# One decoder layer on one core: the order of the value products in attention, and where side b's keys and values lie

## The chip, the cores and the metric

The kernel runs on one core of one Trainium2 chip. The metric is the device time of one execution in microseconds (us); lower is better. Times below come from three timed executions and from one further execution that was profiled. The engines are named as in the profile: PE (TensorE: matmuls; PEld is its weight load), DVE (VectorE), ACT (ScalarE), POOL (GpSimd) and SP (SyncE, which issues the DMAs).

## What is computed

The layer takes 1024 tokens of width 1024. It normalises them, modulates them with a condition vector and projects them with one wide matrix (`w_in`, 5144 columns). Two attentions share the input. **Side a** has 8 heads in 2 groups of 4 that share keys and values; it runs three branches (compressed keys, selected blocks `s`, a window `w` of 512). **Side b** has 8 heads in 2 groups, a window of 128 and a learned sink in the softmax. Their gated outputs are projected, merged, projected again, added to the input and normalised.

```
o_sel = _selected_attention(qa, k_s, v_s, sel_idx)
o_win = _banded_attention(qa, k_w, v_w, NSA_WINDOW)
...
o_b = _banded_attention(qb, k_b, v_b, SWA_WINDOW, sinks[l]).reshape(B, S, SWA_WIDTH)
...
merged = jax.nn.sigmoid(gm_a) * (y_a @ w_up_a[l]) + jax.nn.sigmoid(gm_b) * (y_b @ w_up_b[l])
out = merged @ w_out[l]
```

## The kernel before

The program is written as one stream per stage, and the framework's scheduler then orders the instructions of each engine by its own model of their times. So the order on an engine is not the order in the source.

**Stages.** Until about 145 us of the profiled span the input is normalised and the first projections are made; from there to about 740 us attention runs; then the gates, the two up-projections and the output projection follow.

**Attention** (`Att`, `run` L942 on) goes through 32 units: side a or b, group g, query tile qt of 128 tokens. A unit has one or two branches, a branch a row of key tiles of 128 keys. For each key tile `score` (L887 on) multiplies keys with the queries of 4 heads (two matmuls of 512 columns, `qa` and `qb`), adds a mask on DVE where the tile is an edge (L898), takes the exponentials `e` on ACT (L900, L902), rounds them to 16 bits as `ph` on ACT (L905), and subtracts to get the low part `pl` on POOL (L908). `weigh` (L911) then multiplies the exponentials with the values: for each of 4 heads three small matmuls of 64 or 65 columns, in which `ph` or `pl` is the stationary operand: `ph` with the values' high part, `ph` with their low part, `pl` with the high part. That is 12 matmuls for a key tile, and there are 162 key tiles. `combine` (L922 on) divides and adds up the branches (L930 to L936).

**Fill.** Between these steps `feed` (in `run`) hands out pieces of other projections, called fill below: query projections, the keys and values of side b (`kv_b`), and the gate columns (`gm_block`). Their products write to two PSUM banks (`pj`), which DVE or ACT must empty before the next one starts. All matmuls are issued by the helper `mm`, so they stand under line L107.

**Keys and values.** `new_kv` (L591 on) makes for each branch and each group a tile of keys `K` (fp32, with extra rows that carry masks and the softmax maximum) and a tile of values `V` (16 bits, high and low part and a column of ones). Group 0's tiles for `s` and `w` lie in the pool `kv0`, group 1's in `kv1`. When side a's first 8 units (group 0) are done, `kv_b` (L1261 on) closes `kv0` and opens the pool `kvb` in its place: four new tiles `Kb`, `Vb`, and fixed rows that must be written into them. `block_rows` (L186 on) builds these in a scratch tile `es` (a memset and four affine_selects on POOL, L189 to L196), and `fixed_kv` (L599 on) copies them to both `Kb` and sets the column of ones in both `Vb`. `es` has the tag `vrb`, the same as side b's raw values `vr["b"]` (printed as `vrb`), so the first raw values (L1277) can be written only when the copies from `es` are done. Of the fixed rows, row 80 picks the maximum of the `s` branch from the queries' extra columns; the tile of the `w` branch has a 1 in row 81 only.

Of the kernel before, what the change touches and what calls it, by code (L numbers as in the profile page):

```python
# [7 lines left out]
F32 = mybir.dt.float32  # L8
# [5 lines left out]
OP = mybir.AluOpType  # L14
# [83 lines left out]
class Layer:  # L98
# [492 lines left out]
    def new_kv(self, ps, br, vp):  # L591

        self.K[br] = [p.tile([128, 2, 1024], F32R, name=f"K{br}{g}") for g, p in enumerate(ps)]
        self.V[br] = [p.tile([128, NT, VW], F16, name=f"V{br}{g}") for g, p in enumerate(ps)]
        self.vinv[br] = self.c2.tile([128, 1], F32, name="vinv" + br)
        self.vr[br] = vp.tile([128, NT, 128], F32, name="vr" + br, tag="vr" + br)
        self.vm[br] = vp.tile([128, NT], F32, name="vm" + br)
# [110 lines left out]
class Att:  # L708
# [112 lines left out]
    def M(self, u):  # L821
        L, nc, w = self.L, self.nc, self.w
        side, g, qt = u
        st = self.U[u]
        qa, qbt = st["qa"], st["qbt"]
        brs = self.branches(u)
        mx = w.tile([128, 4, 2, 3], F32, name="mx", tag="mx", bufs=2)
        nc.gpsimd.memset(mx, -3e38)
        if side == "b":
            nc.gpsimd.tensor_copy(mx[:, :, 0, 2], L.sink[:, g * 4:g * 4 + 4])  # L830
        for bi, (br, kts) in enumerate(brs):
            n = 128 * len(kts)
            k0 = 128 * kts[0]
            ns = -(-n // 512)
            cuts = [0] + [min(n, 128 * -(-len(kts) * (i + 1) // ns)) for i in range(ns)]

            groups = []
            for a, b in sorted(zip(cuts, cuts[1:]), key=lambda c: c[0] - c[1]):
                per = 512 // (b - a) if PACK else 1
                groups += [(a, b, range(h, min(4, h + per))) for h in range(0, 4, per)]  # L840
            slots = [0] * 4
            for a, b, hs in groups:
                ps = self.ms.tile()
                for i, h in enumerate(hs):
                    self.last.append(L.mm(ps[:, i * (b - a):(i + 1) * (b - a)], qa[:, h * 128:h * 128 + 128],
                                     L.K[br][g][:, 0, k0 + a:k0 + b], True, True).ins)
                for i, h in enumerate(hs):
                    parts = []
                    if br == "s" and qt >= 4:
                        d = min(b, n - 128)  # L850
                        parts.append((a, d, st["sel"][:, (k0 + a) // 64:(k0 + d) // 64, None].to_broadcast(
                            [128, (d - a) // 64, 64])))
                        if b == n:
                            parts.append((d, b, L.mk[:, 512:640]))
                    elif br == "s" or (br == "w" and qt < 4) or (br == "b" and qt == 0):
                        parts.append((a, b, L.mk[:, 640 - n + a:640 - n + b]))
                    elif br == "w":
                        parts.append((a, b, L.mk[:, a:b]))
                    else:
                        parts.append((a, b, rawap(L.mk, 0, [[512, 2], [1, 128]])))  # L860
                    for c, d, m in parts:
                        if d == c:
                            continue
                        jk = w.tile([128, 512], BF, name="jk", tag="jk")
                        src, o = ps[:, i * (b - a) + c - a:i * (b - a) + d - a], jk[:, :d - c]
                        if len(m.shape) == 3:
                            src = src.rearrange("p (x y) -> p x y", x=m.shape[1])
                            o = o.rearrange("p (x y) -> p x y", x=m.shape[1])
                        nc.vector.tensor_tensor_reduce(o, src, m, 1.0, -3e38, OP.add, OP.max,  # L869
                                                       mx[:, h, bi, slots[h]:slots[h] + 1])  # L870
                        slots[h] += 1
                yield 0.22 * (b - a) * len(hs) / 512
        nc.vector.tensor_reduce(qbt[:, :, 80:82], mx, axis=AX.X, op=OP.max, negate=True)
        if side == "b":
            es = st["es"] = w.tile([128, 2, 4], F32, name="esink", tag="esink", bufs=3)
            nc.gpsimd.tensor_tensor(es[:, 0], L.sink[:, g * 4:g * 4 + 4], qbt.bitcast(F32)[:, :, 80], op=OP.add)
            nc.scalar.activation(es[:, 1], es[:, 0], AF.Exp, bias=L.poff)
        yield 0
        tr = self.ms.tile([128, 4, 128], F32R)
        for h in range(4):  # L880
            self.last.append(nc.tensor.transpose(tr[:, h, :], qbt[:, h, :], L.idr).ins)  # L881
        qb = st["qb"] = w.tile([128, 512], F32R, name="qb", tag="qb", bufs=2)
        nc.scalar.copy(qb, tr.bitcast(F32).rearrange("p h t -> p (h t)"))
        yield 0.25
# [23 lines left out]
        eng.tensor_tensor(pl, e, ph, op=OP.subtract)  # L908
        return ph, pl

    def weigh(self, u, br, kt, first, last, av, ph, pl):  # L911
        L = self.L
        v = L.V[br][u[1]][:, kt, :]
        for h in range(4):
            o = av[:, h * 65:h * 65 + 65]
            hs = slice(h * 128, h * 128 + 128)
            L.mm(o, ph[:, hs], v[:, 0:65], first and h == 0, False)
            L.mm(o[:, 0:64], ph[:, hs], v[:, 65:129], False, False)
            r = L.mm(o, pl[:, hs], v[:, 0:65], False, last and h == 3)
        return r  # L920

    def combine(self, u, bi, av):  # L922
# [19 lines left out]
    def run(self, units, fill, ratio, values):  # L942

        L = self.L
# [30 lines left out]
        steps = []  # L975
# [4 lines left out]
        first = {}  # L980
# [27 lines left out]
        side = "start"  # L1008
# [4 lines left out]
        av = None  # L1013
        si = 0
        emitted = {}
# [7 lines left out]
        for gi, grp in enumerate(groups):  # L1023
            u, bi = steps[grp[0]][:2]
            ui = units.index(u)
            side = "e" if ui < EU else u[0]
            n = ends[ui] - first[u]

            while si <= groups[min(gi + 1, len(groups) - 1)][-1]:
                su = steps[si][0]  # L1030
                finish(self.M, su)
                emitted[si] = self.score(su, steps[si][2], steps[si][3])
                si += 1
                feed(0.43)
            k = grp[-1] - first[u] + 1
            if ui + 1 < len(units):
                part(self.M, units[ui + 1], k, n)
            if ui + 2 < len(units):
                part(self.C, units[ui + 2], k, n)
            if steps[grp[0]][4]:  # L1040
                av = self.av.tile()
            for i in grp:
                br, kt, fst, lst = steps[i][2:]
                w = self.weigh(u, br, kt, fst, lst, av, *emitted.pop(i))
            anchors.append(w.ins)
            feed(0.54 * len(grp))
            if lst:
                self.combine(u, bi, av)
            if k == n:
                if ui + 1 < len(units):  # L1050
                    finish(self.M, units[ui + 1])
                if ui + 2 < len(units):
                    finish(self.C, units[ui + 2])
                self.U.pop(u)
                fill.done(u)
# [51 lines left out]
def run_layer(L):  # L1107
    tc, nc, I = L.tc, L.nc, L.I
# [41 lines left out]
    qp, qp_cm = L.pool("q")  # L1150
# [5 lines left out]
    k1, k1_cm = L.pool("kv1")  # L1156
    k0, k0_cm = L.pool("kv0")
    vp, vp_cm = L.pool("vrows")
# [6 lines left out]
    es = vp.tile([128, 1024], F32, name="es", tag="vrw")  # L1165
# [89 lines left out]
    wk, wk_cm = L.pool("work", 1, side="right")  # L1255
# [3 lines left out]
    kvb = []  # L1259

    def kv_b():  # L1261

        L.close(k0_cm)
        p, cm = L.pool("kvb")
        kvb.append(cm)
        es = p.tile([128, 1024], F32, name="es", tag="vrb")
        L.block_rows(es)
        L.new_kv((p, p), "b", p)
        L.fixed_kv("b", es)
        w = chunk(L.w_in_src(OFF_KVB, 256), 256, eng=lambda: nc.gpsimd)  # L1270
        yield 0
        for t in range(NT):
            a = pj.tile()
            for k in range(KT):
                L.proj(a[:, :256], t, w, ks=[k])
                yield 0.33
            nc.scalar.copy(L.vr["b"][:, t], a[:, 128:256])  # L1277
            L.v_max("b", t)
            L.kv_tail(t, a[:, 0:128], "b", p, A.ms, nc.vector)
        L.v_split("b", A.ms.tile(), p)  # L1280
# [1 line left out]
    fill.kv = kv_b  # L1282
    A.run(units, fill, RATIO, values)
    fill.rest()
    for cm in (wk_cm, kvb[0], k1_cm, qp_cm):
        L.close(cm)


# [3 lines left out]
    wk, wk_cm = L.pool("work2", 2, side="right")  # L1292
# [44 lines left out]
    wk, wk_cm = L.pool("work3", 2, side="right")  # L1337
# [24 lines left out]
    for j in range(KT):  # L1362
        ws = []
        for i, nm in enumerate("ab"):
            src = I["w_up_" + nm].rearrange("l (k p) c -> (l p) k c", p=128)
            w = []
# [133 lines left out]
```

## Time and profile before

| what | value |
|---|---|
| median of 3 timed executions | 966.98 us (966.77 to 968.43) |
| profiled execution, its own time | 970.35 us |
| its span in the profile | 968.6 us |
| PE busy | 932.0 us, 96% of the span |
| POOL, DVE, ACT busy | 607.5, 553.3, 470.9 us |
| matmul instructions in the trace | 6592 |

The profile is of one execution. A matmul's end is modelled, so the start of one matmul to the start of the next tells more than a duration: it is called a slot below. A chain of waits is followed back from the last instruction to what released each step.

### The profile page before, as it was taken

How to read it: one execution, taken by the hardware profiler on the slowest of the kernel's cores; microseconds unless marked ns; L12 is line 12 of the kernel's file. 1: busy time of each engine (PE TensorE's matmuls, PEld its weight loads, DVE VectorE, ACT ScalarE, POOL GpSimd, SP SyncE). 2: the span in 40 equal slices, each digit the busy share in tenths (PEclk: the TensorE clock that was granted, in tenths of full speed). 3: DMA queues.
4: the chain of work that ended last, by engine and by line, in shares of the span. 5: the costliest groups of instructions: out<-in, count | busy, mean ns of one | idle time of the engine just before them, and what ended most of it. 6: DMA issues, size and time to landing. Idle time of an engine off the chain costs nothing.

```text
span 968.6 us, 18679 instructions
## 1 busy us (share of the span) xinstructions
PE 932.0 (96%) x6592; PEld 784.3 (81%) x6592; DVE 553.3 (57%) x1613; ACT 470.9 (49%) x983; POOL 607.5 (63%) x841
## 2 busy tenths in 40 slices
PE   7899999999999999989999999999989989999995
PEld 5789998788898887878899877799768758778885
DVE  7933465544675653466876552455652556554687
ACT  5846334335546556546655466655763544632100
POOL 7867566355758676767777666656753666635733
PEclk8999999999999999999999999999999999999998
DMA  9813222222102122103101222121305948666212
GB/s 333 273 38 113 80 76 71 61 66 78 49 7 62 50 60 67 50 12 88 50 7 40 66 61 66 50 67 39 88 23 186 295 132 244 202 198 223 92 78 97
DMA packets 93278, 95.40 MB, mean 98 GB/s; under 512 B 7616, under 2 KB 72192, under 8 KB 93184
## 3 DMA queue, kind: packets, MB, share of 16 engines
q1 hardware_dynamic: 93184, 94.21, 31.6%
q8 instruction: 52, 0.85, 0.4%
q14 instruction: 42, 0.34, 0.1%
HBM read 73.21 MB, written 20.97 MB: 97 GB/s over the span
## 4 chain that ended last, share of the span: by engine, by line
PE 78%; DVE 6%; POOL 5%; ACT 4%; DMA 4%; issue 3%; POOLq 0%; SPq 0%; DVEq 0%; ACTq 0%
PE bank L107 75%; DMA x<-in_x_dram 1%; POOL rstd L541 1%; DVE res L1433 1%; PE bank L751 1%; PE bank L881 1%; DMA raw<-in_w_up_b_dram 1%; POOL whl L258 1%; POOL pl L908 1%; DMA raw<-in_w_up_a_dram 1%; DMA z<-gm_raw 1%; DVE e L898 1%; DVE stats L1421 1%; DVE z L1420 1%; DVE lnst L531 0%
## 5 line engine op out<-in xcount | busy, mean ns | idle before, releaser
L107 PE MATMUL bank<-whl,uH 128*128 128x256 f32 (+3 forms) x1168 | 271.3, 323 | 5.7 <-ACT uH L448 3.4
L107 PE MATMUL bank<-uH,whl 128*128 128x512 f32 x768 | 252.3, 402 | 0.2 <-DVE cf L931 0.2
L908 POOL TENSOR_TENSOR pl<-e,ph 128x512 f16<-128x512 f32 x162 | 188.5, 1170 | 77.1 <-ACT ph L905 61.1
L107 PEld LDWEIGHTS bank<-whl,uH 128*128 128x128 f32 x1168 | 196.8, 189 | 24.2 <-ACT uH L448 4.4
L107 PE MATMUL bank<-whl,uL 128*128 128x256 f32 (+3 forms) x584 | 182.4, 321 | 0.0
L107 PEld LDWEIGHTS bank<-uH,whl 128*128 128x128 f32 x768 | 141.7, 190 | 27.9 <-PE bank L881 0.5
L107 PE MATMUL bank<-uL,whl 128*128 128x512 f32 x384 | 152.5, 398 | 0.0
L258 POOL TENSOR_TENSOR whl<-raw,whl 128x256 fp32r<-128x256 f32 x128 | 100.2, 791 | 53.6 <-ACT whl L257 46.2
L107 PEld LDWEIGHTS bank<-whl,uL 128*128 128x128 f32 x584 | 109.6, 188 | 8.0
L905 ACT CAST ph<-e 128x512 f16<-128x512 f32 x162 | 98.0, 618 | 28.3 <-PE bank L107 26.2
L869 DVE CUSTOM_DVE_ANT_0 jk<-bank,mk 128x256 bf16<-128x256 f32 (+3 forms) x168 | 73.8, 439 | 32.3 <-PE bank L107 28.9
L902 ACT ACTIVATE e<-bank,poff 128x512 f32<-128x512 f32 x92 | 62.0, 687 | 52.8 <-PE bank L107 45.0
L107 PEld LDWEIGHTS bank<-uL,whl 128*128 128x128 f32 x384 | 72.8, 189 | 15.4
L107 PE MATMUL bank<-yH,whl 128*128 128x512 f32 x256 | 81.9, 402 | 1.7 <-ACT yH L1315 0.8
L257 ACT CAST whl<-raw 128x256 fp32r<-128x256 f32 x128 | 50.9, 402 | 64.8 <-PE bank L107 39.9
L107 PEld LDWEIGHTS <-ph 128*128 128x128 f16 x1296 | 66.1, 97 | 15.1 <-issue 7.6
L898 DVE TENSOR_TENSOR e<-bank,mkt 128x512 f32<-128x512 f32 x70 | 47.5, 688 | 53.1 <-PE bank L107 36.4
L247 POOL TENSOR_TENSOR whl<-raw,whl 128x256 fp32r<-128x256 f32 (+3 forms) x60 | 54.4, 913 | 26.4 <-ACT whl L246 26.2
L107 PEld LDWEIGHTS <-pl 128*128 128x128 f16 x648 | 59.6, 99 | 12.5 <-issue 6.9
L1248 DVE COPY gmo<-bank 128x512 f32<-128x512 f32 x48 | 33.1, 689 | 57.3 <-PE bank L107 50.4
L900 ACT ACTIVATE e<-e,poff 128x512 f32<-128x512 f32 x70 | 49.8, 721 | 32.5 <-DVE e L898 32.3
L246 ACT CAST whl<-raw 128x256 fp32r<-128x256 f32 (+3 forms) x72 | 34.2, 480 | 63.9 <-DMA raw<-in_w_out_dram 35.7
(303 smaller groups left out, 1786.9 us busy)
## 6 DMA issues: line engine op xcount, KB each, us to landing
raw<-in_w_in_dram SPq DMA_DIRECT2D x136, 128.0 KB, 2.2
gm_raw<-gmo SPq DMA_DIRECT2D x48, 256.0 KB, 2.1
wada<-in_w_ada_dram SPq DMA_DIRECT2D x16, 512.0 KB, 6.1
sg<-gm_raw SPq DMA_DIRECT2D x32, 256.0 KB, 3.3
x<-in_x_dram SPq DMA_DIRECT2D x8, 512.0 KB, 5.0
o_raw<-q SPq DMA_DIRECT2D x32, 128.0 KB, 1.9
o<-o_raw SPq DMA_DIRECT2D x8, 512.0 KB, 6.6
z<-gm_raw SPq DMA_DIRECT2D x16, 256.0 KB, 4.9
```

The lines of the kernel that those rows point to most:

```text
L107: return self.nc.tensor.matmul(out, l, r, start=start, stop=stop, skip_group_check=True)
L246: self.cast = nc.scalar.copy(h, raw).ins
L247: low = eng.tensor_tensor(l, raw, h.bitcast(F32), op=OP.subtract).ins
L257: nc.scalar.copy(hl[:, 0], raw)
L258: eng.tensor_tensor(hl[:, 1], raw, hl.bitcast(F32)[:, 0], op=OP.subtract)
L869: nc.vector.tensor_tensor_reduce(o, src, m, 1.0, -3e38, OP.add, OP.max, mx[:, h, bi, slots[h]:slots[h] + 1])
L898: nc.vector.tensor_tensor(e.rearrange("p (h q) -> p h q", h=4), ps.rearrange("p (h q) -> p h q", h=4), L.mkt[:, int(edge), None, :].to_bro ...
L900: nc.scalar.activation(e, e, AF.Exp, bias=L.poff)
L902: nc.scalar.activation(e, ps, AF.Exp, bias=L.poff)
L905: nc.scalar.copy(ph, e)
L908: eng.tensor_tensor(pl, e, ph, op=OP.subtract)
L1248: (nc.scalar.copy if GMC == 2 or GMC == 1 and (b + th) % 2 else nc.vector.tensor_copy)(g, a)
```

## The change

Two things are changed. First, `weigh` takes the list of tiles of a step (here always one), puts for each head the low part `pl` first and then the two products of `ph`, and ties each matmul to follow the one before it (`issue_after`), so that the scheduler keeps the 12 of a key tile together. Second, side b gets no `K` and `V` tiles and no fixed rows of its own: its group 0 uses the tiles of side a's group 0 of branch `s`, and its group 1 those of branch `w`. Since the latter has its 1 in row 81, side b's maximum and sink move to slot `g`. `kv0` stays open to the end of attention, and `kvb` holds the raw values alone, under no shared tag with `es`.

```
+        self.new_v(br, vp)
+
+    def new_v(self, br, vp):
         self.vinv[br] = self.c2.tile([128, 1], F32, name="vinv" + br)
...
-            nc.gpsimd.tensor_copy(mx[:, :, 0, 2], L.sink[:, g * 4:g * 4 + 4])
+            nc.gpsimd.tensor_copy(mx[:, :, g, 2], L.sink[:, g * 4:g * 4 + 4])
...
-    def weigh(self, u, br, kt, first, last, av, ph, pl):
+    def weigh(self, u, br, tiles, first, last, av):
...
+        todo = []
+        for kt, ph, pl in tiles[::-1]:
+            v = L.V[br][u[1]][:, kt, :]
+            for h in range(4):
+                o = av[:, h * 65:h * 65 + 65]
+                hs = slice(h * 128, h * 128 + 128)
+                todo += [(o, pl[:, hs], v[:, 0:65]), (o, ph[:, hs], v[:, 0:65]), (o[:, 0:64], ph[:, hs], v[:, 65:129])]
+        r = None
+        for i, (o, p, v) in enumerate(todo):
+            first_, last_ = first and i == 0, last and i == len(todo) - 1
+            if r is None:
+                r = L.mm(o, p, v, first_, last_)
+            else:
+                with L.tc.issue_after(r.ins):
+                    r = L.mm(o, p, v, first_, last_)
...
-        L.close(k0_cm)
         p, cm = L.pool("kvb")
...
-        es = p.tile([128, 1024], F32, name="es", tag="vrb")
-        L.block_rows(es)
-        L.new_kv((p, p), "b", p)
-        L.fixed_kv("b", es)
+        L.new_v("b", p)
+        L.K["b"], L.V["b"] = ([x[br][0] for br in "sw"] for x in (L.K, L.V))
```

What the scheduler makes of it on two engines. On PE, the start of a key tile's value products in side a's second group, before (`Vs`, `Ks`, `Kw` are values and keys, `qa`, `qb`, `qat` queries, `bank` a PSUM bank):

```order
L107 LDWEIGHTS ph
L107 MATMUL bank_6254<-Vs_931,ph 128x65
L107 LDWEIGHTS ph
L107 MATMUL bank_6254<-Vs_931,ph 128x64
L107 MATMUL bank_6355<-qa,Kw_936 128x512
L107 MATMUL bank_6355<-qb,Kw_936 128x512
L107 MATMUL bank_6296<-Ks_929,qa 128x512
L107 LDWEIGHTS pl
L107 MATMUL bank_6254<-Vs_931,pl 128x65
```

and the same tile with the change:

```order
L754 MATMUL bank_6310<-idr,qat 128x128
L107 LDWEIGHTS pl
L107 MATMUL bank_6237<-Vs_931,pl 128x65
L107 LDWEIGHTS ph
L107 MATMUL bank_6237<-Vs_931,ph 128x65
L107 LDWEIGHTS ph
L107 MATMUL bank_6237<-Vs_931,ph 128x64
```

Before, two products of `ph` stood ahead of other matmuls and the ten others of the tile behind them; now the 12 begin with `pl` and stand in one piece. Over PE's whole order the 1944 value products stood in 186 unbroken runs (57 of them of 2, 49 of 10), and now stand in 131 (82 of 12, 22 of 24); the matmuls are the same 6498 in number.

On POOL, where `kv_b` begins, before (`q` and `qat` queries, `cs` compressed scores, `mx` maxima):

```order
L190 AFFINE_SELECT es<-es 128x1024
L936 TENSOR_TENSOR q<-q,osum 128x256
L192 AFFINE_SELECT es<-es 128x1024
L828 MEMSET mx 128x24
L745 TENSOR_TENSOR qat<-q,qat 128x4x64
L936 TENSOR_TENSOR q<-q,osum 128x256
L194 AFFINE_SELECT es<-es 128x1024
L196 AFFINE_SELECT es<-es 128x1024
L609 CAST Kb_5680<-es 64x1024
L609 CAST Kb_5681<-es 64x1024
L767 TENSOR_TENSOR cs<-cs,csm 128x256
L908 TENSOR_TENSOR pl<-e,ph 128x512
```

and with the change (`kr` and `khl` are side b's rotated keys):

```order
L912 TENSOR_TENSOR pl<-e,ph 128x512 x3
L831 MEMSET mx 128x24
L748 TENSOR_TENSOR qat<-q,qat 128x4x64
L949 TENSOR_TENSOR q<-q,osum 128x256
L284 TENSOR_TENSOR kr_5810<-rope_a,rope_b 128x128
L293 TENSOR_TENSOR khl<-kr_5810,khl 128x2x64
L770 TENSOR_TENSOR cs<-cs,csm 128x256
L949 TENSOR_TENSOR q<-q,osum 128x256
L284 TENSOR_TENSOR kr_5895<-rope_a,rope_b 128x128
```

Nine instructions are gone from POOL (the memset of `es`, its four affine_selects, two copies to `Kb`, two memsets of `Vb`), and the first rotated keys of side b come ahead of the compressed scores. No other engine gains or loses an instruction.

## Rows read from the trace of the kernel before

**Rows 1.** The page: busy time by engine; the chain by engine.
```profile
PE 932.0 (96%) x6592; PEld 784.3 (81%) x6592; DVE 553.3 (57%) x1613; ACT 470.9 (49%) x983; POOL 607.5 (63%) x841
PE 78%; DVE 6%; POOL 5%; ACT 4%; DMA 4%; issue 3%; POOLq 0%; SPq 0%; DVEq 0%; ACTq 0%
```

**Rows 2.** Stretches: us, busy PE, PEld, DVE, ACT, POOL, clock, DMA share, GB/s.
```profile
260.00:310.00 50.00, 50.00 (x482) 45.87 (x481) 35.45 (x141) 25.29 (x49) 35.57 (x48) 1.00 0.12 31
400.00:420.00 20.00, 17.42 (x170) 15.68 (x169) 12.07 (x45) 10.86 (x22) 19.69 (x26) 1.00 0.15 43
700.00:740.00 40.00, 35.84 (x291) 28.21 (x292) 19.13 (x70) 22.43 (x46) 19.55 (x30) 1.00 0.13 35
```

**Rows 3.** Timeline of PE at 204 us: start, length, instruction.
```profile
204.38 0.24 PE L107 MATMUL bank<-Vs,ph 128*128 128x65 f16 x2
204.45 0.47 PE L107 MATMUL bank<-qb,Kw 128*128 128x512 f32 x1
204.77 0.20 PE L107 MATMUL bank<-Vs,pl 128*128 128x65 f16 x1
```

**Rows 4.** Timeline of PE at 309 to 311 us.
```profile
309.56 0.39 PE L107 MATMUL bank<-uH,whl 128*128 128x512 f32 x1
309.79 0.20 PE L107 MATMUL bank<-Vs,pl 128*128 128x65 f16 x1
...
309.90 0.19 PE L107 MATMUL bank<-Vs,pl 128*128 128x65 f16 x1
...
309.99 0.19 PE L107 MATMUL bank<-Vs,pl 128*128 128x65 f16 x1
...
310.45 0.19 PE L107 MATMUL bank<-Vs,pl 128*128 128x65 f16 x1
310.48 0.48 PE L107 MATMUL bank<-qa,Ks 128*128 128x512 f32 x1
310.79 0.40 PE L107 MATMUL bank<-qb,Ks 128*128 128x512 f32 x1
```

**Rows 5.** Timeline of PE at 410.7 us: 128-column products.
```profile
410.70 0.28 PE L107 MATMUL bank<-whl,uL 128*128 128x256 f32 x1
410.81 0.56 PE L107 MATMUL bank<-kcd,qa 128*128 128x128 f32 x4
411.21 0.24 PE L107 MATMUL bank<-Vw,ph 128*128 128x65 f16 x2
```

**Rows 6.** Groups by line and form: count, busy us, mean ns, idle before.
```profile
L107 PEld LDWEIGHTS bank<-uH,whl 128*128 128x128 f32 x768 | 141.7, 190 | 27.9 <-PE bank L881 0.5
L107 PEld LDWEIGHTS <-ph 128*128 128x128 f16 x1296 | 66.1, 97 | 15.1 <-issue 7.6 <-ACT ph L905 2.1 <-ACT e L900 1.0
```

**Rows 7.** The chain of waits at 404 to 415 us: start, length, what.
```profile
404.15 0.97 POOL es L189
...
413.60 1.05 POOL Kb L609
...
414.74 0.61 POOL cs L767
```

**Rows 8.** Timeline of ACT: the first raw values of side b.
```profile
414.69 0.42 ACT L1277 COPY vrb<-bank 128x128 f32<-128x128 f32 x2
```

**Rows 9.** Timeline of PE at 411 to 421 us: idle time before, and its releaser.
```profile
412.91 0.50 PE L107 MATMUL bank<-qa,Kw 128*128 128x512 f32 x1 [0.61 <-ACT e L902]
...
415.88 0.48 PE L107 MATMUL bank<-whl,uH 128*128 128x256 f32 x2 [1.70 <-ACT cs L769]
...
420.73 0.44 PE L799 MATMUL bank<-idf,cp 128*128 128x128 f32 x2 [0.62 <-DVE cp L775]
```

**Rows 10.** Waits of PE's weight loads: total us, times, longest us.
```profile
PEld L107 <- POOL pl L908: 1.7, 7, 0.3
```

**Rows 11.** Stretches at 185 to 195 us, columns as in group 2.
```profile
185.00:190.00 5.00, 3.87 (x23) 2.68 (x21) 3.62 (x13) 4.05 (x8) 1.46 (x2) 0.92 0.31 88
190.00:195.00 5.00, 4.77 (x23) 4.00 (x24) 2.75 (x10) 1.31 (x3) 3.52 (x6) 0.50 0.00 0
```

More of the change, by code (lines that the diff above doesn't have):

```diff
@@ L869, in M @@
                         nc.vector.tensor_tensor_reduce(o, src, m, 1.0, -3e38, OP.add, OP.max,
-                                                       mx[:, h, bi, slots[h]:slots[h] + 1])
+                                                       mx[:, h, g if side == "b" else bi, slots[h]:slots[h] + 1])
                         slots[h] += 1
@@ L875, in M @@
             es = st["es"] = w.tile([128, 2, 4], F32, name="esink", tag="esink", bufs=3)
-            nc.gpsimd.tensor_tensor(es[:, 0], L.sink[:, g * 4:g * 4 + 4], qbt.bitcast(F32)[:, :, 80], op=OP.add)
+            nc.gpsimd.tensor_tensor(es[:, 0], L.sink[:, g * 4:g * 4 + 4], qbt.bitcast(F32)[:, :, 80 + g], op=OP.add)
             nc.scalar.activation(es[:, 1], es[:, 0], AF.Exp, bias=L.poff)
@@ L909, in score @@
         return ph, pl
-    def weigh(self, u, br, kt, first, last, av, ph, pl):
+    def weigh(self, u, br, tiles, first, last, av):
         L = self.L
[L913 to L919, printed above, removed]
+        todo = []
[13 more added lines that the diff above has]
+                    r = L.mm(o, p, v, first_, last_)
         return r
@@ L1041, in run @@
                 av = self.av.tile()
-            for i in grp:
-                br, kt, fst, lst = steps[i][2:]
-                w = self.weigh(u, br, kt, fst, lst, av, *emitted.pop(i))
+            br, fst, lst = steps[grp[0]][2], steps[grp[0]][4], steps[grp[-1]][5]
+            w = self.weigh(u, br, [(steps[i][3], *emitted.pop(i)) for i in grp], fst, lst, av)
             anchors.append(w.ins)
@@ L1284, in run_layer @@
     fill.rest()
-    for cm in (wk_cm, kvb[0], k1_cm, qp_cm):
+    for cm in (wk_cm, kvb[0], k0_cm, k1_cm, qp_cm):
         L.close(cm)
```

## The prediction
> **What bounds the kernel now.** I read the page first. PE is busy for 96% of the span and makes 78% of the chain that ended last [rows 1], so the kernel is bound by PE's own work, and a change counts if it shortens PE's work or takes away a wait of PE. Next I read the stretches, to see where PE is not full [rows 2]. In the middle of attention it is busy for 50.00 of 50 us. At 400 to 420 us it is busy for 17.42 of 20, while POOL is busy for 19.69; at 700 to 740 us for 35.84 of 40, with no other engine near full. So there are three kinds of time: PE-bound, a place where POOL is full, and an end of attention where each unit waits for the one before it through PE, DVE, ACT and POOL in turn. The two parts of the change fall into the first two.
>
> Then I read PE's timeline for slots, since a busy PE need not be a fast one. A product of 512 columns has a slot of 0.23 us (309.56 to 309.79) [rows 4]. Within a run of value products three starts lie within 0.09 us (309.90 to 309.99), so 0.03 us each [rows 4]. But the first 512-column product behind such a run has a slot of 0.31 us (310.48 to 310.79) [rows 4], and behind a run of only two it is 0.32 us (204.45 to 204.77) [rows 3]. The trace has 104 such places with 512 columns, of which these are two, and the middle case costs 0.084 us; products of 256 columns pay the same 0.084 in their 29 cases. My explanation: the next stationary operand is loaded while the current matmul runs, and a load of fp32 weights is longer than a value product of 0.03 us, so it shows. The records fit: an fp32 load is given 190 ns, a 16-bit load of `ph` 97 [rows 6]. Entering a run costs next to nothing (0.009 us in the middle case).
>
> **Part 1, the runs.** The change neither adds nor removes a matmul. It turns 186 unbroken runs into 131, so 55 times the 0.084 us behind a run and the 0.009 us at its head are saved. Seven of the 55 lie among the last 18 of the 162 key tiles, where PE waits for others anyway; I count them at nothing, since there the chain through ACT and POOL covers them (if that cover is gone they give 0.6 us more). 48 x 0.093 = 4.5 us. Against it: fp32 loads also show behind products of 128 columns. Four of these take 0.40 us (410.81 to 411.21), 0.10 each, where half of a 256-column slot of 0.11 (410.70 to 410.81) would be 0.06 [rows 5]; the new order has 8 more such places at some 0.05, so 0.4 us is lost. **Part 1 gives 4.1 us**, with bounds of 0 and 5.7 (all 55, and nothing lost behind the transposes).
>
> Here a rule of the Trainium skill speaks against the change. The Trainium skill (TensorE: Matmul & The Clock Gate, section "LDWEIGHTS (loading the stationary operand)") gives a weight load as columns / 1.2 ns, whatever the type, which by an estimate from that page is 107 ns for each load here. By it a value product would expose its load wherever it follows another value product, a run would cost as much inside as behind it, and part 1 would be 0. The trace disagrees with that for 16 bits, 0.03 us from start to start [rows 4]; the Trainium skill has on that same page, section "Weight-path perf modes", a faster load for types other than fp32, which fits.
>
> **Part 2, POOL where side b's keys begin.** Nine POOL instructions go. In the chain of waits at 404 to 415 us seven of them stand one behind another, from the memset of `es` (0.97) to the second copy to `Kb` (1.05), about 7.0 us together, with `pl` and others between [rows 7]. What hangs on them: the first raw values of side b are written at 414.69, within 0.05 us of the end of the last copy (413.60 + 1.05), since `es` and `vrb` are one buffer [rows 7, 8]. Until then the PSUM bank of `kv_b`'s projection is not emptied, so PE has no fill, and whatever it then waits for shows: 0.61, 1.70 and 0.62 us of idle time [rows 9]. With the change the raw values wait for no scratch tile, the compressed scores (`cs`, 414.74 [rows 7]) wait behind no block of 7 us, and the fill goes on. The bound above is all three idle times, 2.9 us, for a busy POOL that frees its 7 us is worth no more than the idle time of PE. The bound below is 0: side b's keys now overwrite tiles of side a's group 0, so their copies wait for its last reads; but `kv_b` begins only when those units are done, as before. I take **2.5 us**: the 1.70 is the direct follower of the block, the 0.61 is a wait for an exponential that fill would cover, and a part of the 0.62 (a chain of small DVE and POOL steps) should stay. The mask rows and the shift of the maximum to slot `g` change no size and cost nothing: the same instructions on the same engines.
>
> **Moved and not counted.** `pl` in front means that a run starts when POOL has made the low part, some 0.06 us of matmuls later than with `ph` in front. The other engines keep their instructions, but the scheduler has placed nearly all of attention anew. A shift of a few waits by some us either way is the noise of this forecast. No DMA is added or removed.
>
> **Sum.** 4.1 + 2.5 = 6.6 us. The profiled execution took 970.35 us and would take 963.7; the median of the timed ones is 966.98, 3.4 below it, so I put the same difference there: **960.4 us**, 0.7% less.
>
> **Rivals.**
>
> *Loads cost the same inside a run (chance 0.06).* If what shows behind a run is not the load but something that any change of operand pays, part 1 is 0 and only part 2 is left: 966.98 - 2.5 = 964.5. The steady 0.03 inside runs [rows 4] speaks against it. (The Trainium skill's rule above is this case.)
>
> *Replanning eats the gain (0.14).* The new order moves the wait elsewhere in attention: 4 to 7 us come back as other waits of PE, for instance if the places at 400 to 420 us merely shift to where side b's keys are transposed. That gives 965 to 967.5. For it: the order is made from modelled times. Against it: outside 400 to 420 and the end, PE hardly waits, so there is much slack on the other engines.
>
> *Slower: PE stands at the head of the runs (0.09).* Before, two products of `ph` went first in 57 places and other work stood between them and the first `pl`. Now a run's first matmul needs `pl`, the last thing made, and all that stands behind it on PE waits with it, scores of the next key tile included, from which the next `pl` is made. If POOL is later on the chip than planned, each of 131 runs stands. The point from which this decides is 6.6 / 131 = 0.05 us of mean wait; at 0.1 us it costs 13.1 and the time is 966.98 - 6.6 + 13.1 = 973.5. For it: POOL is busier than ACT and DVE, and full at 400 to 420 us [rows 1, 2]. Against it: today the weight loads wait for `pl` in only 7 places, 1.7 us in all, at most 0.3 [rows 10], and the planner placed `pl`'s products by the same model.
>
> *More than forecast (0.11).* The clock of PE was at half (1.2 of 2.4 GHz) at 190 to 195 us, after PE had been busy for only 3.87 of the 5 us before [rows 11]. By the two rows that was at least 5.8 us (5 and 0.08 x 2 x 5). If the new order fills that place, half of it, 2.9 us, is won besides; with the end of attention shortened as well the time is some 956 to 957.5. The new order leaves that place nearly as it was, so it is unlikely; an extra fall of the clock would cost as much.
>
> **How the numbers follow.** The forecast has 0.60: a gain of 4.5 to 9 us, 958 to 962.5. Two executions of one program differ by some 0.2% (1.9 us), which is what a measurement of this kernel can tell from no change. Faster by more than that (under 965.0) are the forecast, the larger gain and the case of equal loads: 0.60 + 0.11 + 0.06 = 0.77. Within 0.2% is most of the replanning case, 0.14; slower is the head of the runs, 0.09. The range leaves out the slower rival and about half of the larger gain and of the upper edge: 955.0 to 966.5.
>
> **What would show it.** Right: the groups of value products keep their counts, and the slot behind a run stays at 0.31 for 512 columns; there are some 131 such places; `es` and its copies are gone from POOL after 100 us; PE is busy for over 19 us of the 20 in which `kv_b` begins, and its projections are not held back; from 430 us on everything comes some 4 us earlier, and at the end of attention some 6 to 7. Wrong: weight loads that wait for `pl` for over 6 us in all; new idle times of PE of a microsecond or more in attention; or a stretch of half clock where there was none.

## The result, and the profile after

| what | before | with the change |
|---|---|---|
| median of 6 timed executions each, same chip | 967.70 us (966.75 to 970.54) | 960.65 us (959.10 to 962.07) |
| ratio | 1 | 0.9922, 95% interval 0.9910 to 0.9935 |
| profiled execution, its span | 970.35, 968.6 us | 960.47, 958.7 us |

The change makes the kernel 0.78% faster, 7.5 us by the ratio (the two medians lie 7.05 us apart). The forecast was 960.4 us in a range of 955.0 to 966.5: time and sign came out. Whether its two terms did is the matter of the runs below.

The page of the changed kernel, busy time by engine and the chain by engine, as in [rows 1]:

```profile
PE 923.9 (96%) x6592; PEld 784.5 (82%) x6592; DVE 553.1 (58%) x1613; ACT 471.1 (49%) x983; POOL 600.3 (63%) x832
PE 80%; DVE 7%; DMA 4%; POOL 4%; ACT 3%; issue 2%; POOLq 0%; DVEq 0%; ACTq 0%
```

POOL has lost its nine instructions and 7.2 us; the matmuls are the same 6592. Its stretches, columns as in [rows 2] (busy PE, PEld, DVE, ACT, POOL, then the granted clock):

```profile
400.00:420.00 20.00, 20.00 (x206) 19.20 (x205) 13.52 (x55) 12.32 (x28) 15.27 (x23) 1.00 0.05 15
700.00:740.00 40.00, 37.72 (x260) 30.27 (x259) 13.43 (x41) 16.51 (x32) 16.45 (x21) 1.00 0.34 115
185.00:190.00 5.00, 3.74 (x22) 2.48 (x19) 3.59 (x14) 4.05 (x8) 1.34 (x2) 1.00 0.36 97
190.00:195.00 5.00, 4.75 (x33) 4.04 (x34) 3.15 (x11) 1.31 (x3) 3.61 (x6) 1.00 0.00 0
```

PE is full where `kv_b` begins (17.42 of 20 us before), and POOL no longer is. At 700 to 740 us the two kernels are at different points of their work, so the 37.72 is no gain by itself. The half clock of [rows 11] is not there in this execution.

PE's timeline behind a run of 24 value products:

```profile
307.02 0.19 PE L107 MATMUL bank<-Vs,pl 128*128 128x65 f16 x1
307.05 0.22 PE L107 MATMUL bank<-Vs,ph 128*128 128x65 f16 x2
307.11 0.48 PE L107 MATMUL bank<-qa,Ks 128*128 128x512 f32 x1
307.43 0.40 PE L107 MATMUL bank<-qb,Ks 128*128 128x512 f32 x1
307.66 0.39 PE L107 MATMUL bank<-qa,Ks 128*128 128x512 f32 x1
```

The slot behind a run is still 0.32 us (307.11 to 307.43), the next 0.23, and the run still steps by 0.03, as in [rows 3] and [rows 4]; only the places are fewer. Summed over attention from the traces, what the slots behind runs take above the usual slot (the median of the other products of their width) was 13.5 us in 182 places and is 9.8 us in 129.

The groups of weight loads, as in [rows 6]:

```profile
L107 PEld LDWEIGHTS <-ph 128*128 128x128 f16 x1296 | 64.7, 97 | 0.8 <-issue 0.5
L107 PEld LDWEIGHTS <-pl 128*128 128x128 f16 x648 | 59.2, 98 | 16.0 <-issue 10.3 <-POOL pl L912 1.3 <-POOL whl L247 0.6
```

The wait of these loads for `pl`, as in [rows 10]:

```profile
PEld L107 <- POOL pl L912: 1.3, 5, 0.4
```

Part of the idle time of the weight loads has moved: ahead of `ph` it fell from 15.1 us to 0.8, but ahead of `pl`, which is now at the head, it rose from 12.5 us to 16.0. The wait for `pl` is 1.3 us in 5 places (1.7 in 7 before). The rival that PE would stand at the head of the runs did not happen.

ACT's timeline, the first raw values of side b and the split of its values, `kv_b`'s last step:

```profile
402.38 0.27 ACT L1287 COPY vrb<-bank 128x128 f32<-128x128 f32 x1 [0.24 <-PE bank L107]
461.53 0.73 ACT L332 ACTIVATE Vs<-vrb,vmxb 128x512 f16<-128x512 f32 x1
```

The raw values come 12.3 us earlier than in [rows 8] and the split 7.5 us earlier than before (468.98); of both, some 3 us are before's half clock at 190 us [rows 11], which this execution lacks. Before was not shown in these stretches, so here it is, columns as above:

```profile
400.00:426.00 26.00, 22.80 (x229) 20.80 (x228) 15.82 (x59) 12.90 (x28) 24.20 (x33) 1.00 0.11 33
426.00:475.00 49.00, 48.74 (x360) 41.95 (x359) 33.98 (x114) 24.90 (x61) 29.73 (x45) 1.00 0.23 63
```

PE idles for 3.20 us in the first and 0.26 in the second, which spans the rest of `kv_b`. These two numbers are followed through all runs.

### The profile page after: what moved, and what is told of

The parts are those of the page before. It is cut to its first block, busy times and chain, and to the rows that moved or that the text cites. A ratio compares the mean times of both kernels' runs of the same rounds, so it can differ in the third digit from the quotient of the medians.

```text
span 958.7 us, 18660 instructions
## 1 busy us (share of the span) xinstructions
PE 923.9 (96%) x6592; PEld 784.5 (82%) x6592; DVE 553.1 (58%) x1613; ACT 471.1 (49%) x983; POOL 600.3 (63%) x832
## 4 chain that ended last, share of the span: by engine, by line
PE 80%; DVE 7%; DMA 4%; POOL 4%; ACT 3%; issue 2%; POOLq 0%; DVEq 0%; ACTq 0%
PE bank L107 77%; DMA z<-gm_raw 1%; DMA x<-in_x_dram 1%; POOL rstd L541 1%; DVE res L1443 1%; DVE jk L873 1%; PE bank L885 1%; PE bank L754 1%; DMA raw<-in_w_up_b_dram 1%; POOL whl L258 1%; POOL zsg L1319 1%; DVE stats L1431 1%; DVE z L1430 1%; DVE e L902 1%; DVE lnst L531 0%
## 5 line engine op out<-in xcount | busy, mean ns | idle before, releaser
L107 PE MATMUL bank<-uH,whl 128*128 128x512 f32 x768 | 249.1, 398 | 0.2
L107 PEld LDWEIGHTS bank<-yH,whl 128*128 128x128 f32 x256 | 48.0, 190 | 14.6 <-ACT yH L1325 1.5
```

Of the source, the lines that this page charges most:

```text
L107: return self.nc.tensor.matmul(out, l, r, start=start, stop=stop, skip_group_check=True)
```

## The experiments

All ratios are to the kernel before on the same chip. "Clock" is the mean granted clock over the timed executions (before: 0.9906 to 0.9913), and "idle" is PE's at 400 to 426 and at 426 to 475 us of the profiled one. The last column is the time from the start of the 600th of the 1944 value products to the start of the 1200th, read from PE's timeline: it holds all of `kv_b` and compares the same work, whatever was gained or lost ahead of it (1523 matmuls with the old order of products, 1520 with the new).

| kernel | products | side b's tiles | ratio (95%) | clock | idle, us | raw values, split, us | 600th to 1200th, us |
|---|---|---|---|---|---|---|---|
| before | old | own | 1 | 0.991 | 3.20, 0.26 | 414.7, 469.0 | 175.1 |
| e1 | new | own | 0.9995 (0.9986 to 1.0004) | 0.9886 | 3.62, 0.04 | 416.2, 467.1 | 176.4 |
| e2 | old | shared | 0.9946 (0.9932 to 0.9961) | 0.9935 | 0, 0.26 | 403.7, 463.0 | 170.9 |
| e15, as e2 | old | shared | 0.9959 (0.9944 to 0.9974) | 0.9908 | 0, 0.26 | 404.5, 463.9 | 170.9 |
| the change | new | shared | 0.9922 (0.9910 to 0.9935) | 0.9922 | 0, 0.59 | 402.4, 461.5 | 169.4 |
| e13, as the change | new | shared | 0.9933 (0.9917 to 0.9949) | 0.9927 | 0, 0.59 | 405.1, 464.3 | 169.4 |
| e12 | old | own, no block | 1.0015 (1.0005 to 1.0025) | 0.9892 | 0.29, 2.02 | 405.7, 470.3 | 176.4 |
| e14 | new | own, no block | 0.9989 (0.9976 to 1.0002) | 0.9910 | 0.91, 1.82 | 402.3, 466.2 | 174.9 |
| e10 | new | shared, block | 0.9959 (0.9945 to 0.9973) | 0.9927 | 0, 2.21 | 403.4, 465.6 | 173.2 |
| e11 | new | shared, block, link | 1.0055 (1.0039 to 1.0070) | 0.9848 | 6.49, 0.36 | 421.6, 475.6 | 181.9 |

**Each part alone.** e1 keeps the new `weigh` and gives side b its own tiles again:

```
+        es = p.tile([128, 1024], F32, name="es", tag="vrb")
+        L.block_rows(es)
+        L.new_kv((p, p), "b", p)
+        L.fixed_kv("b", es)
-        L.new_v("b", p)
-        L.K["b"], L.V["b"] = ([x[br][0] for br in "sw"] for x in (L.K, L.V))
```

> Only the order of the value products is changed; side b keeps its own tiles and fixed rows. The built order has 128 unbroken runs against 186 before. Theory (an fp32 load shows behind each run, 0.084 us): about 4.2 us less than before, ratio about 0.9957, and the 2.9 us of idle time of PE where kv_b begins stay. Rival (a load costs the same inside a run): no gain, ratio 1.000. Rival (the clock's missing fall at 189 us is the gain): about 3 us less only if the granted clock shows no fall near 189 us.

Measured: 0.9995, a miss. Part 1 alone is worth 0.5 us (-0.4 to 1.4) of the 4.1. Its stretches, columns as above:

```profile
400.00:410.00 10.00, 8.97 (x102) 7.84 (x98) 5.10 (x22) 5.65 (x12) 9.90 (x15) 1.00 0.05 15
410.00:420.00 10.00, 7.41 (x57) 5.60 (x57) 7.03 (x25) 3.28 (x8) 9.15 (x12) 0.70 0.04 13
```

What its PE waits for at 400 to 426 us (total us, times, longest):

```profile
PE bank L799 <- DVE cp L775: 1.2, 1, 1.2
PE bank L107 <- POOL pl L908: 0.8, 1, 0.8
```

POOL is full (9.90 of 10 us) and the first raw values come at 416.2, so PE meets the same wait earlier in its work and idles 3.62 us, 0.4 more than before. `pl` is now one of the things waited for. What differs more is the clock: 0.70 at 410 to 420, where before has 1.00 from 400 to 475 us. PE from 150 us to the last value product, before and e1, columns as above:

```profile
150.00:736.32 586.32, 575.67 (x4789) 486.92 (x4788) 327.04 (x1172) 320.17 (x647) 384.38 (x522) 0.99 0.19 54
150.00:732.84 582.84, 571.09 (x4786) 488.23 (x4786) 326.99 (x1171) 320.85 (x647) 384.32 (x521) 0.99 0.19 54
```

The saving itself is there, for the slots behind runs take 9.5 us above the usual in 123 places. But attention ends only 3.5 us earlier, and 2.7 of these are before's half clock at 190 us (the lead that e2, with the same order up to there, has at the 400th value product). Of the 4.3 us of busy time that the new order saves where the tiles are shared (below), 0.8 are left: 1.1 come back as idle time (10.65 to 11.75 us) and some 2.4 as busy time, an estimate from these rows, which fits the stretch of low clock. In the timed executions too the mean clock is lower, 0.9886 against 0.9913. How much that costs over all executions is open: 0.0027 of 968 us would be 2.6 us, but among the 65 executions of the kernel before that were timed beside these runs, 0.01 of clock goes with only some 2.3 us, which makes 0.6.

e2 is the reverse: the old `weigh` with the shared tiles.

```
-            w = self.weigh(u, br, [(steps[i][3], *emitted.pop(i)) for i in grp], fst, lst, av)
+            for i in grp:
+                br, kt, fst, lst = steps[i][2:]
+                w = self.weigh(u, br, kt, fst, lst, av, *emitted.pop(i))
```

> Only side b's keys and values move into side a's first group's tiles; the value products have the old order, 186 runs. Theory: about 2.5 us less than before, ratio about 0.9974, PE full at 400 to 420 us, and e1 and e2 together give the whole gain of 7 us. Rival (replanning noise): within 1 us of before and no idle time regained.

> The same kernel as e2_tiles_only, once more, to tell how far the size of the second part alone holds. Theory: 0.9946 again, within 0.9925 to 0.9965, so about twice the 2.5 us of the forecast; and the stall at 400 to 426 us is gone in this execution too. Rival: the first run was lucky with the clock, and the ratio is 0.9965 to 0.998 (2 to 3.4 us), with half clock in stretches where e2_tiles_only had none.

Measured: 0.9946, and 0.9959 when the same kernel ran again. The mean, 0.9953, is 4.6 us, nearly twice the 2.5 of the forecast and 2.1 us over the first expectation. Its stretches:

```profile
400.00:426.00 26.00, 26.00 (x277) 24.89 (x277) 18.45 (x73) 12.38 (x30) 17.23 (x26) 1.00 0.11 32
426.00:475.00 49.00, 48.74 (x358) 41.48 (x356) 34.53 (x123) 29.39 (x66) 33.32 (x48) 1.00 0.25 70
```

The whole 3.20 us is gone and nothing comes back behind it. By the last column of the table e2 and e15 both gain 4.1 us at `kv_b`, and after it their distance to before stays as it is to the end of attention. Of the 4.1, 3.2 are idle time (3.46 to 0.26). The other 0.9 is busy time of PE at a clock of 1.00 in all three executions; where it goes was not followed, but the clock it is not.

**The change again**, as e13, to see how far one result reaches.

> The change once more, beside the three others on the same chip, for a direct comparison and a second profile. Ratio to before 0.992 as measured. If the time goes with the stretches of half clock, an execution with 3.4 us more of them is about 1.7 us longer; the stage of the gates (48 to 51 us in the profiles so far) should differ between the two profiles of this same program by as much as between programs.

Measured: 0.9933. The mean of the two, 0.9928, against 0.9953 for e2 and e15 gives part 1 2.4 us where the tiles are shared (1.0 to 3.8, from the intervals). PE from 150 us to the last value product, e2 and the change, columns as above:

```profile
150.00:729.45 579.45, 571.88 (x4790) 484.90 (x4789) 326.42 (x1171) 320.35 (x647) 376.91 (x512) 1.00 0.19 54
150.00:726.27 576.27, 567.60 (x4791) 487.01 (x4790) 326.33 (x1172) 320.46 (x647) 377.81 (x513) 1.00 0.19 54
```

PE's busy time falls by 4.3 us, which is the price of the loads as forecast. Its idle time rises by 1.1, from 7.57 to 8.67 us (7.43 in e15, 8.65 in e13), and 0.9 of that lies behind 480 us, where attention ends. So 3.2 us are left in these traces, within the interval of the timed ones.

**The price of a load, by itself.** e9 leaves out the whole layer and its output is filler: PE alone, products of 512 columns with fp32 weights (`bb`), of 65 columns with 16-bit weights (`ba`), and mixes, each tied to the one before.

```
+        for _ in range(40):
+            small(12)
+            big()
...
+        for _ in range(40):
+            small(12)
+            mm(bb, w16, x16)
...
+        for _ in range(40):
+            for _ in range(4):
+                mm(ba[:, 0:128], w32, x32[:, 0:128])
+            big()
```

> Not the layer: PE alone, no waits, with constant operands; the output is not the layer's. Stretches of 40 times: 12 products of 65 columns with 16-bit weights and then one of 512 with fp32 weights; 2 and one; 480 small ones without a break; 12 small ones and one of 512 with 16-bit weights; four products of 128 columns with fp32 weights and one of 512; one of 128 and one of 512. Theory (what shows is the fp32 load, as long as the product ahead of it does not cover it): the 512-column slot is 0.232 us alone, 0.31 behind 12 and behind 2 small ones alike, 0.22 to 0.24 where its weights are 16-bit, about 0.28 behind a product of 128 columns; small ones 0.03 each. Rival (any change of type or shape costs): 0.31 also with 16-bit weights. Rival (a load takes the same for each type): small ones 0.1 each.

PE's timeline in e9 (start, length, instruction, times):

```profile
20.23 0.48 PE L103 MATMUL bb<-x,w 128*128 128x512 f32 x1
20.55 0.54 PE L103 MATMUL ba<-x,w 128*128 128x65 f16 x12
...
46.71 5.02 PE L103 MATMUL bb<-x,w 128*128 128x512 f32 x21
51.57 0.24 PE L103 MATMUL ba<-x,w 128*128 128x65 f16 x2
...
100.16 0.38 PE L103 MATMUL bb<-x,w 128*128 128x512 f16 x1
100.38 0.52 PE L103 MATMUL ba<-x,w 128*128 128x65 f16 x12
100.74 0.38 PE L103 MATMUL bb<-x,w 128*128 128x512 f16 x1
...
125.38 0.44 PE L103 MATMUL bb<-x,w 128*128 128x512 f32 x1
125.66 0.56 PE L103 MATMUL ba<-x,w 128*128 128x128 f32 x4
126.05 0.45 PE L103 MATMUL bb<-x,w 128*128 128x512 f32 x1
```

A 512-column fp32 product takes 0.32 us behind small ones (20.23 to 20.55) and 0.23 among its like (46.71 to 51.57 is 4.86 us for 21, the first of them behind small ones). With 16-bit weights the same place takes 0.22 (100.16 to 100.38), and the 12 small ones 0.36, 0.03 each. There both operands are 16-bit, so these rows alone could also mean a price for a change of type. The last rows speak against that: among fp32 products alone a 512-column one takes 0.28 us behind one of 128 columns (125.38 to 125.66), and those of 128 take 0.10 each. So 0.09 us is the price of an fp32 load that a product of 0.03 us can't cover, and not of a change of operand. The Trainium skill (TensorE: Matmul & The Clock Gate, section "LDWEIGHTS (loading the stationary operand)") gives one load time, by the columns alone; the 0.32 against 0.22 is against it. The rival of equal loads is out.

**The block and the link, put back.** e6 and e8 add to the change a POOL block of the size of the one removed, which nothing reads: e6 in scratch of its own (832 columns, and one copy more), e8 in the buffer of the raw values. The lines of e8:

```
+        es = p.tile([128, 1024], F32, name="es", tag="vrb")
+        nc.gpsimd.memset(es, 1.0)
+        for base in (64 * 64, 63 - 64 * 64, 79, 80):
+            nc.gpsimd.affine_select(es, es, pattern=[[1, 1024]], compare_op=OP.is_ge, fill=0.0, base=base,
+                                    channel_multiplier=-64)
+        for i in range(2):
+            nc.gpsimd.tensor_copy(es[64:128, :], es[64:128, :])
```

> The change, with POOL work of the removed block's length (a memset, four affine_selects, three copies on 832 columns) put back on a scratch tile of its own that nobody waits for; the shared buffer with the raw values is not put back. Theory A (the wait on the shared buffer made the idle time): within 1 us of the change, ratio to before 0.992 to 0.993. Theory B (POOL's time itself made it): about 2.5 us slower than the change, ratio 0.995.

> As the run before, with the scratch tile in the buffer of the raw values again (1024 columns, two copies), so that the first raw values wait for it. PE's built order is the same as in that run. Theory A: 2 to 3 us slower than that run, idle time of PE of 2 to 3 us where kv_b begins is back, ratio to before about 0.995. Theory B: as that run, within 1 us.

Measured: 0.9963 (0.9949 to 0.9977) and 0.9926 (0.9912 to 0.9939). Neither tested what was meant: with no closed pool to wait for, the block ran at 167 to 180 us, long before `kv_b`. e8 lost nothing by it; why e6 was 3.6 us slower than e8 was not followed, but it is not `kv_b`: from the 600th to the 1200th value product both take 169.4 us, as the change does. So in e10 (scratch of its own) and e11 (the buffer of the raw values) the block first reads the ones of `Vs` and `Vw`, which side a's last products hold back:

```
+        es = p.tile([128, 832], F32, name="es", tag="esb")
+        for br in "sw":
+            nc.gpsimd.memset(L.V[br][0][:, :, 64:65], 1.0)
+            nc.gpsimd.tensor_copy(es[:, 0:8], L.V[br][0][:, :, 64])
+        nc.gpsimd.memset(es, 1.0)
...
```

> The change, with POOL work of the removed block's length put back where it stood before: on a scratch tile of its own, held back until the last value products of side a's group 0 have read their tiles, with nobody waiting for it. Theory A (what cost was the wait of the raw values for the scratch tile): within 1.5 us of the change, ratio to before about 0.993. Theory B (POOL's 7 us themselves cost): 3 to 4 us slower than the change, 0.996 to 0.997.

> As the run before, with the scratch tile in the buffer of the raw values, so that these wait for the block. Theory A: PE is idle again for 3 to 6 us in the 20 us in which kv_b begins, the clock falls there in part of the executions, and the time is near that of the runs alone, ratio 0.997 to 1.000. Theory B: as the run before.

Measured: 0.9959 and 1.0055, against 0.9933 for the change on the same chip. In place, the block costs 2.5 us and the link 9.3 us more. e6, with the same scratch, is about as slow in all (0.9963), but loses its time elsewhere: its first value product starts 3.3 us later than the change's (193.9 against 190.6 us), and from the 600th to the 1200th it takes 169.4 us, where e10 takes 173.2. So e10's loss at `kv_b` is one of the block's place and not of the scratch. The stretches of e10:

```profile
400.00:426.00 26.00, 26.00 (x272) 25.04 (x270) 17.40 (x65) 13.44 (x31) 23.35 (x34) 1.00 0.05 16
426.00:475.00 49.00, 46.79 (x324) 37.79 (x324) 32.38 (x114) 26.35 (x60) 30.36 (x45) 1.00 0.22 63
```

The stretch of e11, then ACT's timeline and what PE waits for there:

```profile
400.00:426.00 26.00, 19.51 (x183) 15.64 (x181) 14.60 (x52) 10.92 (x21) 20.61 (x26) 0.82 0.08 26
```

```profile
421.55 0.43 ACT L1297 COPY vrb<-bank 128x128 f32<-128x128 f32 x2 [2.79 <-POOL es L1287]
```

```profile
PE bank L107 <- POOL pl L912: 1.8, 2, 1.2
```

Without the link the raw values start on time and PE stays full beside a full POOL (23.35 of 26 us); it idles later, 2.21 us. With it they wait for the block (2.79 us of idle ACT, released by `es`), PE loses its fill, idles 6.49 us, and the clock falls (0.82; 0.66 over 415 to 435 us). Of the 12.5 us that e11 takes more than the change from the 600th to the 1200th product, 6.3 are idle time, and the rest fits the low clock; so the 9.3 us are the price of the wait and of the clock behind it. That is the wait of [rows 7 to 9], larger than there because the block here starts later.

**Block and link gone, tiles kept apart.** e12 is the kernel before without `es`: side b has its own tiles, and the fixed rows are copied from side a's group 1.

```
-        es = p.tile([128, 1024], F32, name="es", tag="vrb")
-        L.block_rows(es)
         L.new_kv((p, p), "b", p)
-        L.fixed_kv("b", es)
+        for g in range(2):
+            nc.gpsimd.memset(L.V["b"][g][:, :, 64:65], 1.0)
+            nc.gpsimd.tensor_copy(L.K["b"][g][64:128, 1, :], L.K["s"][1].bitcast(F32)[64:128, 1, :])
```

> The kernel before with one thing changed: side b's tiles stay its own, but their fixed rows are copied from side a's group 1 (two copies, two memsets), so the scratch tile, its memset and its four affine_selects are gone and the raw values wait for nothing. Value products in the old order (189 runs). Theory A: most of the gain of the tiles alone, ratio 0.994 to 0.997, and no idle time of PE over 1 us where kv_b begins. Rival (what helps is that side b's tiles no longer need kv0's place to be free): no gain, 0.999 to 1.001.

Measured: 1.0015. By the forecast's reason this had to give the 2.5 us, and it gave none. Its stretches:

```profile
400.00:426.00 26.00, 25.71 (x255) 24.53 (x254) 16.28 (x64) 13.03 (x30) 19.79 (x30) 1.00 0.11 32
426.00:475.00 49.00, 46.98 (x333) 38.18 (x333) 32.91 (x111) 25.29 (x59) 28.30 (x44) 0.99 0.22 63
466.00:472.00 6.00, 4.56 (x23) 2.97 (x21) 5.83 (x24) 3.27 (x8) 2.69 (x7) 1.00 0.31 81
470.00:480.00 10.00, 8.85 (x56) 6.75 (x55) 7.77 (x33) 7.83 (x15) 4.82 (x7) 0.83 0.06 15
```

The chain of waits there (start, length, what):

```profile
465.95 0.42 DVE Kb L306
466.37 0.64 DVE jk L869
...
467.63 0.43 DVE Kb L308
468.05 0.50 DVE p L782
...
471.14 0.56 DVE jk L869
```

The first rotated keys on POOL's timeline, and what ACT's has after them:

```profile
407.91 0.45 POOL L284 TENSOR_TENSOR kr<-rope_a,rope_b 128x128 f32<-128x128 f32 x1
```

```profile
409.99 0.27 ACT L1277 COPY vrb<-bank 128x128 f32<-128x128 f32 x1 [1.83 <-PE bank L107]
...
414.63 0.29 ACT L292 CAST khl<-kr 128x128 fp32r<-128x128 f32 x1
```

The wait at 400 us is gone (0.29 us) and the raw values start 9.0 us earlier. But `kv_b` ends no earlier (split at 470.3; 469.0 before), and PE idles 2.02 us at 426 to 475 instead. There DVE is full, 5.83 of 6 us: the last key copies (L306, L308), the maxima (`jk`) and the choice of blocks (`p`) follow one another on it, with PE behind them. And behind that stall the clock falls, to 0.83 at 470 to 480 us, where before has 1.00: the idle time of both stretches together is 1.15 us less than before, yet the same work takes 1.4 us longer (176.4 against 175.1). The rival of the expectation, that side b's tiles need `kv0`'s place to be free, is not what holds `kv_b` up: both `Kb` take their fixed rows at 403.7 and 405.0 us. The first rotated keys (`kr`) are there at 408.4, and ACT is idle until 409.99, yet rounds them (L292) only at 414.63: the order on ACT holds them back, not a wait. In e2 the same step comes 2.4 us after the first raw values, here 8.9. Why the scheduler spreads `kv_b` so where the tiles are separate was not settled.

**The new order of products on top of it.** e14 is e12 with the change's `weigh`.

> The kernel of e12_rows_copied with the change's order of value products: side b keeps tiles of its own, the fixed rows are copied from side a's group 1, and no scratch tile stands in the way. 131 runs of value products in place of 189. Theory 'the runs pay only where the POOL block is gone': the wait in front of the first raw values is gone, as in e12_rows_copied (1.0015 of before), so the runs now give what they give on top of the shared tiles, 2.4 us or more: 0.994 to 0.999 of before, and PE's stalls of over 0.25 us at 400 to 426 us stay under 1 us. Rival 'the runs pay only with the shared tiles, whatever stands at 400 us': the time stays within 0.2% of e12_rows_copied, 1.000 to 1.003 of before, because PE again arrives earlier at a wait that some other step sets (in e12_rows_copied 3.7 us of stalls at 467 to 474 us), and these stalls grow to 6 us or more.

Measured: 0.9989 (0.9976 to 1.0002), at the upper edge of the first theory. Against e12 the runs give 0.0026, 2.5 us (0.9 to 4.1, from the intervals), the same as with shared tiles, though e14 idles about as long at 426 to 475 (1.82 us). The first theory holds by both of its marks, though the interval reaches just past its edge: the time was gained, and the stall at 400 us did not grow past 1 us (0.91). The rival's later stall did not grow at all.

**Longer runs.** e7 sets two key tiles to a step: 115 runs instead of 131.

```
-GRP = 1
-PB, EB = 3, 2
+GRP = 2
+PB, EB = 4, 2
```

> The change, with two key tiles of a branch in one step (four buffers for ph and pl in place of three). The built order has 115 runs against 131, and 12 more fp32 loads behind 128-column products. Theory: 16 x 0.093 less 0.6, about 0.9 us less than the change, ratio to before about 0.991. Rival (longer runs hold back the next scores, above all at the end of attention): 1 to 4 us slower than the change.

Measured: 0.9964 (0.9950 to 0.9978), slower than the change. From 150 us to the last value product PE idles for 11.5 us, and for 8.7 with the change; the clock is 0.9885 in its timed executions. What fewer runs save is lost to waits.

No version here beats the change; e8 equals it. One part of the diff does nothing: the built order of every engine is the same without `issue_after`. So putting `pl` first is what keeps the 12 products together.

## Why the prediction was right or wrong

- **The sum, 6.6 us, and the time, 960.4: right** (7.5 and 960.65), but partly by luck: part 1 gave less than its term and part 2 more, and the two errors offset each other.
- **Part 1, the price: right.** 0.31 to 0.32 us behind a run, 0.23 elsewhere, 0.03 inside, in the change and in e9 alone; PE's busy time in attention falls by 4.3 us, 4.1 forecast. **As a gain in time it was mis-sized**: 2.4 us by the timed executions and 3.2 by the traces, on top of part 2. The step that failed was to count the places as time won because PE idles in few of them: PE idles 1.1 us more with the new order, most of it at the end of attention, where the forecast had put the seven last places at nothing and not at a loss. Alone (e1) the gain is 0.5 us, for PE then meets the block sooner, and the clock falls behind that wait in the profiled execution. Part 1's worth depended on part 2, and the two were added as if they did not touch.
- **Part 2: mis-sized, and its reason half right.** 2.5 forecast with 2.9 as the bound above, 4.6 measured alone, 4.1 by the traces. That block and link hold PE up where `kv_b` begins is shown by e10 and e11 (2.5 us, and 9.3 more with the clock's fall). That the bound above is the three idle times of [rows 9] failed twice. PE idles 3.46 us from 400 to 475 before and 0.26 in e2, so 3.2 us; and 0.9 us of busy time goes besides, at an equal clock, from a cause that stays open. And taking block and link away is not enough (e12): the wait goes on to a full DVE, and the clock falls behind it. What the shared tiles bring besides is an order in which the split of side b's values comes 3.3 us earlier (e2 and e15: 6.0 and 5.1, less the lead of 2.7 and 1.8 that these executions had ahead of `kv_b`).
- **Slips in the numbers, without weight for the result.** The bound of 5.7 for part 1 counts the seven last places twice: 55 x 0.093 is 5.1. Replanning that gives back 4 us would end at 964.4, not 965. The larger gain, at 956 to 957.5, lies within the stated range and is not left out by half.
- **Rivals.** Equal loads: out (e9). Replanning: 1.1 us of idle time in the change and not 4 to 7; in full it is what e12 does. Waits for `pl` at the head of the runs: not in the change (1.3 us); they do appear where POOL is full (0.8 us in e1, 1.8 in e11). More than forecast, by the clock at 189 us: that half clock is missing in the change's first profile and present in its second, so it is no effect of the change.
- **"From 430 us on some 4 us earlier, 6 to 7 at the end of attention": right**, once like is set beside like. e13's execution has the half clock at 190 us as before's has: its split is 4.7 us earlier and its last value product 7.3 us (729.0 against 736.3 us). In the change's first profile, which lacks it, they are 7.5 and 10.0 us earlier (726.3).

## What to carry to other kernels

Price a saving of the bound engine only together with the next wait it runs into: the same new order was worth 2.4 us with the wait out of the way and 0.5 with it there. Where a stall of the bound engine is removed, ask which engine is full a little later, and look whether the scheduler's order brings the released work forward at all. Scratch that shares a buffer with the first output of a stage turns the scratch's whole chain into a wait of that stage; in a buffer of its own the same block cost 2.5 us where it cost 11.8 with the link, the fall of the clock behind the wait included. And before two profiles are compared, look whether both have the same stretches of half clock: here that alone moved every later time by some 2.7 us.

## What was not expected of the hardware

The granted clock differs between executions of one program at one place. This is e13, the same kernel as the change, in the stretches shown above for the change:

```profile
185.00:190.00 5.00, 3.81 (x22) 2.53 (x20) 3.59 (x15) 4.05 (x8) 1.28 (x2) 0.95 0.35 98
190.00:195.00 5.00, 4.68 (x24) 4.01 (x25) 2.84 (x10) 1.30 (x3) 3.71 (x6) 0.50 0.00 0
```

PE was busy for 3.81 of the 5 us ahead and went to half clock (1.2 of 2.4 GHz); in the change's first profile it was busy for 3.74 and stayed at 1.00. So the loss at such a place is a chance and not a fixed term, and one profile can't tell whether a change removed it.
